# Splitting the last 344 tokens of a hybrid encoder layer into two parts of 172

## The chip, the cores and the metric

The kernel runs on one core of one Trainium2 chip, as one program. The metric is the device time of that program in microseconds (us); lower is better. The core has five engines that run side by side and wait for each other by semaphores: TensorE (PE, matrix products; its weight loads are shown apart as PEld), VectorE (DVE), ScalarE (ACT), GpSimd (POOL) and SyncE (SP, which here issues every transfer between HBM and the core). Products are written to eight banks of accumulator memory, each 128 partitions by 512 fp32 numbers.

## The reference, cut to what matters

One layer of an encoder trunk on 2048 prompt tokens and 32 sample tokens, model width 1024. The change touches only the very end of it, the second product of the feed-forward block, the residual sum and the final norm:

```
h = rmsnorm(x, norm_ffn_g) * (1 + sc2) + sh2
x = x + gt2 * (square(relu(h @ w_up)) @ w_down)      # w_up 1024 x 4096, w_down 4096 x 1024
y = rmsnorm(x, final_norm_g)

def rmsnorm(x, g):
    return x * rsqrt(mean(x * x, axis=-1) + 1e-6) * g
```

## The kernel before, in words

**Layout.** Everything is kept transposed: the 1024 model columns lie on the 128 partitions in eight tiles (`m` = 0 to 7), tokens run along the free axis. The feed-forward stage walks over three blocks of tokens (`b`), each made of two groups `g`. In the last block a group has 344 tokens; group 1 holds the end of the sequence with the 32 sample tokens, group 0 the 344 tokens before that. Group 1 is worked first, group 0 last, so it is group 0 that ends the program. Sums of the second product are kept in `acc[m][g]`.

**Precision by three products.** A fp32 operand is split into a high and a low part (`hi`, `lo`) of type fp32r, and a product is made of three matmuls (`mm3`, line 427, recorded by `mms`, profile line L414): high weights by high values, high by low, low by high. Each has its own load of a 128x128 tile of weights, even where two in a row use the same tile: 16000 loads for 16000 matmuls in the page.

**The hidden columns.** The 4096 hidden columns are taken in eight rounds `q`. Rounds before the last use a seven-product scheme; the last round of the last block (`ffn_last`, line 1875) is done plainly: for each group, each of the eight output tiles is the sum of 4 products of 3 matmuls, 12 matmuls of 344 columns, in one bank.

**After each output tile.** VectorE multiplies the bank by the gate and adds the sum so far (`stt`, L373); ScalarE squares it (`act`, L353); the squares of the tiles are added up into one tile (in group 0 by VectorE, `tt`, L368), except that for group 0 the squares of the last two tiles are kept apart.

**The last norm** (`final`, line 1936, and `rms_row`, line 859). The sum over the partitions is made on TensorE with the tile of squares as weights and a column of ones as values: a group of 344 is three pieces of 128 tokens, and each piece of each tile of squares shows up as two instructions, since here full fp32 is used. Three tiles of squares give 18 instructions. VectorE then scales the 128x3 result (`rcol`, L382), GpSimd raises it to the power of -0.5 (L368, POOL), TensorE turns each column back into a row over all partitions (`tr`, L425), and VectorE multiplies the eight tiles, already scaled by the norm's weights on ScalarE, by that row straight out of the bank. Tiles go out in three pairs and two single tiles (`dma`, L406).

**Banks.** `take` pops a bank from the front of a list of eight and `give` puts it back at the end. Following all calls from the start, the list stands at 1, 2, 0, 3, 6, 4, 5, 7 when `ffn_last` begins, and again when group 0 begins. The row sums and the row that comes back use the ring `M`, which holds bank 7 alone. Bank 7 is so the bank of the eighth output tile of each group, too.

**Order of work.** The program is recorded as a list of operations with what each reads and writes. A planner (`schedule`, line 246) then plays it through with an assumed cost for each operation, an assumed latency between engines, and a priority, and writes out a fixed order for each engine. Of the operations that are ready by its clock it takes the one with the lowest priority number (`LOCAL` 2, `EVAC` 3, which is the default, `GEMM` 4), and among equals the one that a later matmul needs first. Engines follow that order on the chip, whatever the real durations are. The assumed cost of one `mm3` is 3 * (0.443 n + 5) ns for n columns:

```python
self.mms([...], 3 * (0.443 * ps.n + 5))
```

Of the kernel before, what the change touches and what calls it, by code (L numbers as in the profile page):

```python
# [10 lines left out]
AF = mybir.ActivationFunctionType  # L11
ALU = mybir.AluOpType
# [4 lines left out]
P = 128  # L17
D = 1024
KT = 8
# [12 lines left out]
GB = [348, 348, 344]  # L32
FT = [0, 696, 1392]
G = 348
NB = 3
# [8 lines left out]
PE, DVE, ACT, POOL, DMA, NONE = range(6)  # L44
# [13 lines left out]
CHAIN, INV, LOCAL, EVAC, GEMM, IDLE = range(6)  # L58
# [280 lines left out]
class Kern:  # L339
# [1534 lines left out]

    def ffn_last(self, b, q, ops):

        w = {}
        for g, u in ((1, 0), (1, 1), (0, 0), (0, 1)):
            if u not in w:
                w[u] = [self.operand(self.wr, self.raw(self.raws, self.i["w_d"][2 * q + u, x])) for x in range(4)]  # L1880
            for i in range(2):
                for j in range(2):
                    m = 4 * i + 2 * u + j
                    ps = self.take(GB[b])
                    for e in range(2):
                        wh, wl = w[u][2 * i + e]
                        for k in range(2):
                            c = slice(256 * k + 128 * j, 256 * k + 128 * j + 128)
                            with self.p.at(GEMM):
                                self.mm3(ps[1], wh[:, c], wl[:, c], *ops[(e, g)][k], e == k == 0, e == k == 1)  # L1890
                    self.add(b, q, m, g, ps[1], last=True)
                    self.give(ps)
            if u == 1:
                self.final(b, g, self.ssq[g][1:])
        yield

    def ffn_plain(self, b, q, ops):

        for u in range(2):
            w = [self.operand(self.wr, self.raw(self.raws, self.i["w_d"][2 * q + u, x])) for x in range(4)]  # L1900
            for g in range(2):
                for i in range(2):
                    for j in range(2):
                        m = 4 * i + 2 * u + j
                        ps = self.take(GB[b])
                        for e in range(2):
                            wh, wl = w[2 * i + e]
                            for k in range(2):
                                c = slice(256 * k + 128 * j, 256 * k + 128 * j + 128)
                                with self.p.at(GEMM):  # L1910
                                    self.mm3(ps[1], wh[:, c], wl[:, c], *ops[(e, g)][k], e == k == 0, e == k == 1)
                        self.add(b, q, m, g, ps[1], first=True, last=True)
                        self.give(ps)
            if q == 7 and u == 1:
                for g in range(2):
                    self.final(b, g, self.ssq[g][1:])
            yield

    def square(self, b, m, g):

        end = (b, g) == (NB - 1, 0)
        a = self.acc[m][g][:, : GB[b]]
        if self.ssq[g] is None or self.ssq[g][0] != b:
            sa = self.piece("fs", b)
            self.ssq[g] = [b, sa]
            self.act(sa, a, AF.Square)
            return
        x = self.piece("fp" if end and m == 7 else "fx", b)
        self.act(x, a, AF.Square)
        sa = self.ssq[g][1]  # L1930
        if end and m in (6, 7):
            self.ssq[g].append(x)
        else:
            self.tt(sa, sa, x, ALU.add, DVE if end else POOL)

    def final(self, b, g, sq):
        w, ts = GB[b], self.span(b, g)
        end = (b, g) == (NB - 1, 0)
        if end:
            for m in range(KT):  # L1940
                a = self.acc[m][g][:, :w]
                self.act(a, a, AF.Copy, scale=self.nrm[:, 2, m : m + 1])
        r = self.rms_row(sq, w, None if end else sq[0])
        for m in range(KT):
            a, n = self.acc[m][g][:, :w], self.nrm[:, 2, m : m + 1]
            with self.p.at(GEMM):
                if end:
                    if m % 2 == 0:
                        y = self.slot((25, 26, 22, 23)[m // 2], 0, (P, 2, w))
                    self.tt(y[:, m % 2], a, r, ALU.mult)  # L1950
                    if m > 5:
                        self.dma(self.o["yT"][m, :, ts], y[:, m % 2])
                    elif m % 2:
                        self.dma(self.o["yT"][m - 1 : m + 1, :, ts].rearrange("m p t -> p m t"), y)
                    continue
                if m % 2 == 0 and (b < NB - 1 or m < 6):
                    self.tt(a, a, r, ALU.mult, POOL)
                    self.act(a, a, AF.Copy, scale=n)
                else:
                    self.stt(a, a, n, r, ALU.mult, ALU.mult)  # L1960
                with self.p.at(LOCAL):
                    self.dma(self.o["yT"][m, :, ts], a)
# [66 lines left out]
```

## Time and profile before

| | us |
|---|---|
| median of 3 runs | 2316.39 |
| lowest, highest | 2314.38, 2317.95 |
| the profiled execution, its own time | 2321.28 |
| its span, first to last instruction | 2319.5 |
| granted TensorE clock, mean | 0.996 |
| share of TensorE, VectorE, ScalarE, GpSimd in the span | 99%, 72%, 53%, 26% |

Rows of the timeline read: start in us from the span's start, duration in us, engine, line, operation, output <- input by the program's names, shape, how many were merged into the row (x), and in brackets how long the engine stood idle before and what ended it. `f` is a bank of the feed-forward products, `M` the bank of the row sums, `s` a working tile. Rows of groups read: line, engine, operation, names, shape, count, then busy us and mean ns of one. The matmul rows of the feed-forward stage all have one line, L414, so they are told apart by names and shapes.

### The profile page before, as it was taken

What the parts mean: (1) busy time and instruction counts of PE and PEld (TensorE: products, weight loads), DVE (VectorE), ACT (ScalarE), POOL (GpSimd) and SP (SyncE); (2) the same over time, 40 slices, a digit from 0 to 9 for tenths busy, and PEclk for the clock granted to TensorE, in tenths of its full rate; (3) what the DMA queues carried; (4) which work ended last, traced back from release to release, by engine and by line L of the source; (5) the groups of instructions that cost most, each with busy time, mean ns of one, the idle gap of its engine ahead of it and who ended that gap; (6) DMA issues with size and microseconds to landing.
All of it is one profiled execution on the core that took longest, in us unless ns stands there. A gap on an engine that the chain in (4) does not pass through costs nothing.

```text
span 2319.5 us, 45744 instructions
## 1 busy us (share of the span) xinstructions
PE 2294.0 (99%) x16000; PEld 2176.6 (94%) x16000; DVE 1664.7 (72%) x3618; ACT 1220.3 (53%) x2801; POOL 600.2 (26%) x846
## 2 busy tenths in 40 slices
PE   9999999999999999999999999999999999999998
PEld 6877778999999988999999999999999999999998
DVE  6656766577755545689999989776668886666775
ACT  5655656465664434476565545753344564344344
POOL 1124533224334023445444424210000250000001
PEclk9999999999999999999999999999999999999999
DMA  9488778465566766888777786997667897666771
GB/s 328 164 276 284 241 244 242 148 214 175 181 190 192 248 196 207 284 279 275 261 256 253 251 268 222 352 310 238 216 216 251 261 304 228 222 218 217 243 225 54
DMA packets 358328, 547.08 MB, mean 236 GB/s; under 512 B 66425, under 2 KB 182285, under 8 KB 358097
## 3 DMA queue, kind: packets, MB, share of 16 engines
q1 hardware_dynamic: 358096, 544.16, 72.3%
q8 instruction: 126, 2.06, 0.4%
q14 instruction: 106, 0.86, 0.1%
HBM read 390.96 MB, written 153.05 MB: 235 GB/s over the span
## 4 chain that ended last, share of the span: by engine, by line
PE 82%; DVE 6%; DMA 6%; ACT 2%; issue 2%; POOL 2%; SPq 1%; POOLq 0%; DVEq 0%; ACTq 0%
PE f L414 47%; PE g L414 25%; PE C L414 3%; DVE s L368 2%; PE L L414 2%; PE B L414 2%; DVE s L373 2%; ACT s L353 1%; POOL s L368 1%; PE M L414 1%; DVE wl L368 1%; DMA s<-th_d 1%; PE L L425 1%; DMA wr<-w_b 1%; SPq L406 1%
## 5 line engine op out<-in xcount | busy, mean ns | idle before, releaser
L353 ACT ACTIVATE s<-s 128x348 fp32r<-128x348 f32 (+13 forms) x1067 | 492.0, 485 | 333.6 <-DVE s L368 126.8
L414 PE MATMUL f<-s,wh 128*128 128x348 f32 (+1 forms) x2768 | 662.2, 322 | 0.3 <-DVE s L368 0.2
L414 PEld LDWEIGHTS f<-s,wh 128*128 128x128 f32 x2768 | 480.8, 188 | 2.6 <-DVE s L368 1.7
L368 DVE TENSOR_TENSOR s<-f,s 128x348 f32<-128x348 f32 (+1 forms) x696 | 348.2, 512 | 172.2 <-PE f L414 170.7
L414 PE MATMUL f<-s,wl 128*128 128x348 f32 (+1 forms) x1384 | 444.7, 321 | 0.0
L414 PE MATMUL g<-BH,wh 128*128 128x384 f32 (+2 forms) x1088 | 399.2, 367 | 0.7 <-ACT BH L353 0.4
L414 PE MATMUL g<-BH,wl 128*128 128x384 f32 (+2 forms) x1088 | 382.3, 351 | 0.0
L414 PE MATMUL g<-BL,wh 128*128 128x384 f32 (+2 forms) x1088 | 381.1, 350 | 0.4 <-DVE BL L373 0.4
L368 DVE TENSOR_TENSOR s<-s,s 128x348 fp32r<-128x348 f32 (+8 forms) x674 | 348.5, 546 | 37.5 <-ACT s L353 11.1
L414 PE MATMUL f<-BH,wh 128*128 128x348 f32 (+1 forms) x1024 | 330.0, 322 | 2.5 <-DVE s L373 1.9
L414 PE MATMUL f<-BL,wh 128*128 128x348 f32 (+1 forms) x1024 | 330.9, 323 | 0.0
L414 PE MATMUL f<-BH,wl 128*128 128x348 f32 (+1 forms) x1024 | 329.3, 322 | 0.0
L353 ACT ACTIVATE wh<-s 128x512 fp32r<-128x512 f32 x282 | 176.1, 632 | 233.6 <-PE f L414 199.9
L368 POOL TENSOR_TENSOR s<-s 64x15 f32<-64x15 f32 (+12 forms) x328 | 165.4, 504 | 465.1 <-issue 380.4
L368 POOL TENSOR_TENSOR s<-s,s 128x512 f32<-128x512 f32 (+5 forms) x153 | 191.0, 1257 | 289.9 <-ACT s L353 139.8
L414 PEld LDWEIGHTS f<-s,wl 128*128 128x128 f32 x1384 | 260.4, 188 | 0.0
L368 DVE TENSOR_TENSOR wl<-s,wh 128x512 fp32r<-128x512 f32 x282 | 220.2, 789 | 40.1 <-ACT wh L353 39.8
L414 PEld LDWEIGHTS g<-BH,wh 128*128 128x128 f32 x1088 | 205.1, 189 | 22.2 <-issue 3.6
L414 PEld LDWEIGHTS g<-BL,wh 128*128 128x128 f32 x1088 | 205.6, 189 | 17.4 <-DVE BL L373 1.1
L414 PEld LDWEIGHTS g<-BH,wl 128*128 128x128 f32 x1088 | 204.6, 188 | 18.2
L373 DVE SCALAR_TENSOR_TENSOR s<-s,s,s 128x384 f32<-128x384 f32 (+4 forms) x314 | 162.3, 538 | 54.7 <-ACT s L353 27.3
L414 PEld LDWEIGHTS f<-BH,wh 128*128 128x128 f32 x1024 | 192.9, 188 | 3.2 <-DVE s L373 2.2
(133 smaller groups left out, 3332.9 us busy)
## 6 DMA issues: line engine op xcount, KB each, us to landing
s<-w_u SPq DMA_DIRECT2D x124, 256.0 KB, 3.8
s<-w_d SPq DMA_DIRECT2D x121, 256.0 KB, 3.5
wh<-su_d SPq DMA_DIRECT2D x114, 256.0 KB, 3.9
wl<-su_d SPq DMA_DIRECT2D x114, 256.0 KB, 4.0
wh<-sd_d SPq DMA_DIRECT2D x100, 256.0 KB, 3.3
wl<-sd_d SPq DMA_DIRECT2D x100, 256.0 KB, 3.8
wr<-w_b SPq DMA_DIRECT2D x36, 512.0 KB, 5.4
s<-adaw SPq DMA_DIRECT2D x32, 512.0 KB, 6.1
```

Of the source, the lines that this page charges most:

```text
L353: self.p.op(ACT, c, lambda: nc.scalar.activation(out=R(out), in_=R(in_), func=func, **{k: R(v) for k, v in kw.items()}), [out, accum], [in ...
L368: self.p.op(eng, c, lambda: e.tensor_tensor(out=R(out), in0=R(a), in1=R(b), op=op), [out], [a, b])
L373: self.p.op(DVE, c, lambda: nc.vector.scalar_tensor_tensor(out=R(out), in0=R(a), scalar=R(s), in1=R(b), op0=op0, op1=op1), [out], [a, s, b])
L406: self.p.op(DMA, max(500, x), lambda: nc.sync.dma_start(out=R(out), in_=R(in_)), [out], [in_], lat=DMA_LATENCY + min(0, x - 500))
L414: nc.tensor.matmul(R(out), R(l), R(r), **kw)
L425: self.p.op(PE, 114, lambda: nc.tensor.transpose(R(out), R(in_), R(ident)), [out], [in_, ident])
```

## The change

In the last round of the last block, group 0 is no longer worked as 344 columns but as two parts of 172, one after the other: all eight output tiles of part A (tokens 0 to 171 of the group), then all eight of part B (172 to 343). Each part has its own squares, its own row sums and its own norm (`finish`), so it has 8 x 12 matmuls of 172 columns, and TensorE loads the same weight tiles once for each part. In each part the squares of all tiles but the last are added into one tile, and the last tile's square is kept apart, so there are two tiles of squares, each in two pieces (128 and 44 new tokens). Before part A begins, the list of eight banks is divided: the first four, 1, 2, 0, 3, become the ring `M` for the row sums, the other four, 6, 4, 5, 7, serve the products. The weights of both halves are requested ahead of the loop. Group 1 is worked as before.

```diff
-        for g, u in ((1, 0), (1, 1), (0, 0), (0, 1)):
...
+        w = [[self.operand(self.wr, self.raw(self.raws, self.i["w_d"][2 * q + u, x])) for x in range(4)] for u in range(2)]
+        for g, o, n in ((1, 0, GB[b]), (0, 0, 172), (0, 172, 172)):
+            sq = []
+            if (g, o) == (0, 0):
+                self.fbanks, self.banks["M"] = self.fbanks[4:], self.fbanks[:4]
+            for u, i, j in ((u, i, j) for u in range(2) for i in range(2) for j in range(2)):
+                m = 4 * i + 2 * u + j
+                ps = self.take(n)
...
+                        with self.p.at(GEMM):
+                            self.mm3(ps[1], wh[:, c], wl[:, c], hi[:, o : o + n], lo[:, o : o + n], e == k == 0, e == k == 1)
+                if g:
                     self.add(b, q, m, g, ps[1], last=True)
+                else:
+                    x = self.acc[m][0][:, o : o + n]
+                    self.stt(x, ps[1], self.modc[:, 5, m, 0:1], x, ALU.mult, ALU.add)
+                    t = self.new(("fk" if o else "fs") if not sq else "fr" if o else "fp" if m == 7 else "fx", (P, n))
+                    self.act(t, x, AF.Square)
+                    if sq and m != 7:
+                        self.tt(sq[0], sq[0], t, ALU.add)
+                    else:
+                        sq.append(t)
+                self.give(ps)
+            if g:
                 self.final(b, g, self.ssq[g][1:])
+            else:
+                self.finish(o, n, sq)
         yield
+
+    def finish(self, o, n, sq):
+        t0 = FT[NB - 1] + o
+        for m in range(KT):
+            x = self.acc[m][0][:, o : o + n]
+            self.act(x, x, AF.Copy, scale=self.nrm[:, 2, m : m + 1])
+        r = self.rms_row(sq, n, None)
+        for m in range(KT):
+            with self.p.at(GEMM):
+                if m % 2 == 0:
+                    y = self.slot((25, 26, 22, 23)[m // 2], 2 * o, (P, 2, n))
+                self.tt(y[:, m % 2], self.acc[m][0][:, o : o + n], r, ALU.mult)
+                if m > 5:
+                    self.dma(self.o["yT"][m, :, t0 : t0 + n], y[:, m % 2])
+                elif m % 2:
+                    self.dma(self.o["yT"][m - 1 : m + 1, :, t0 : t0 + n].rearrange("m p t -> p m t"), y)
```

What `square` and `final` did for group 0 of the last block (the branches on `end`) is taken out of them.

More of the change, by code (lines that the diff above doesn't have):

```diff
@@ L1875, in ffn_last @@
     def ffn_last(self, b, q, ops):
-        w = {}
-        for g, u in ((1, 0), (1, 1), (0, 0), (0, 1)):
[L1879 to L1890, printed above, removed]
-                    self.add(b, q, m, g, ps[1], last=True)
-                    self.give(ps)
-            if u == 1:
+        w = [[self.operand(self.wr, self.raw(self.raws, self.i["w_d"][2 * q + u, x])) for x in range(4)] for u in range(2)]
@@ new lines, in ffn_last @@
+        for g, o, n in ((1, 0, GB[b]), (0, 0, 172), (0, 172, 172)):
[5 more added lines that the diff above has]
+                ps = self.take(n)
+                for e in range(2):
+                    wh, wl = w[u][2 * i + e]
+                    for k in range(2):
+                        c = slice(256 * k + 128 * j, 256 * k + 128 * j + 128)
+                        hi, lo = ops[(e, g)][k]
+                        with self.p.at(GEMM):
+                            self.mm3(ps[1], wh[:, c], wl[:, c], hi[:, o : o + n], lo[:, o : o + n], e == k == 0, e == k == 1)
+                if g:
+                    self.add(b, q, m, g, ps[1], last=True)
+                else:
[9 more added lines that the diff above has]
+            if g:
@@ L1919, in square @@
     def square(self, b, m, g):
-        end = (b, g) == (NB - 1, 0)
         a = self.acc[m][g][:, : GB[b]]
@@ L1927, in square @@
             return
-        x = self.piece("fp" if end and m == 7 else "fx", b)
+        x = self.piece("fx", b)
         self.act(x, a, AF.Square)
         sa = self.ssq[g][1]
[L1931 to L1934, printed above, removed]
+        self.tt(sa, sa, x, ALU.add, POOL)
     def final(self, b, g, sq):
         w, ts = GB[b], self.span(b, g)
[L1938 to L1943, printed above, removed]
+        r = self.rms_row(sq, w, sq[0])
         for m in range(KT):
@@ L1946, in final @@
             with self.p.at(GEMM):
[L1947 to L1955, printed above, removed]
                 if m % 2 == 0 and (b < NB - 1 or m < 6):
```

## The prediction

> **What bounds the kernel now.** I read the page's first part, then the chain of work that ended last in order of time, then busy time by stretches, then the timeline of the last 30 us.
>
> ```profile
> span 2319.5 us, 45744 instructions
> PE 2294.0 (99%) x16000; PEld 2176.6 (94%) x16000; DVE 1664.7 (72%) x3618; ACT 1220.3 (53%) x2801; POOL 600.2 (26%) x846
> ```
> ```profile
> 2149.94 144.15 PE f L414 x913
> ...
> 2312.91 2.54 DVE s L368 x6
> ```
> ```profile
> 2290.60:2306.90 16.30, 16.29 (x107) 15.98 (x105) 11.08 (x20) 9.40 (x19) 5.67 (x6) 1.00 0.25 88
> 2306.90:2319.50 12.60, 3.19 (x21) 2.71 (x21) 4.21 (x10) 1.34 (x3) 0.86 (x1) 0.60 0.32 112
> ```
>
> See that TensorE sets the pace until about 2307 and that then a chain of small steps runs alone: in the last stretch no engine is busy for more than 4.21 of 12.60 us (columns: PE, PEld, DVE, ACT, POOL, then granted clock). The chain's 144 us piece is products of the feed-forward stage, its last piece the multiplications of the norm. Both stretches are touched by the change: group 0's products, and the chain behind them.
>
> ```profile
> 2290.62 0.47 PE L414 MATMUL f<-s,wh 128*128 128x344 f32 x2
> ```
> ```profile
> 2293.92 0.72 PE L414 MATMUL M<-ones,s 128*128 128x1 f32 x6
> 2296.96 0.49 PE L425 MATMUL M<-ident,rcol 128*128 128x128 f32 x3
> 2297.21 0.56 PE L414 MATMUL f<-s,wh 128*128 128x344 f32 x2
> 2297.49 0.46 ACT L353 ACTIVATE s<-M 128x344 f32<-128x344 f32 x1 [0.44 <-PE M L425]
> ```
> ```profile
> 2306.57 0.32 PE L414 MATMUL f<-s,wl 128*128 128x344 f32 x1
> 2306.93 0.57 DVE L373 SCALAR_TENSOR_TENSOR s<-f,modc,s 128x344 f32<-128x344 f32 x1 [0.90 <-PE f L414]
> 2307.54 0.49 ACT L353 ACTIVATE s<-s 128x344 f32<-128x344 f32 x1 [0.37 <-DVE s L373]
> 2307.55 2.21 PEld L414 LDWEIGHTS M<-ones,s 128*128 128x128 f32 x18 [0.95 <-DVE s L373]
> 2309.89 0.16 DVE L382 TENSOR_SCALAR rcol<-M 128x3 f32<-128x3 f32 x1 [2.38 <-PE M L414]
> 2310.13 0.86 POOL L368 TENSOR_TENSOR rcol<-rcol,mhalf 128x3 f32<-128x3 f32 x1 [8.84 <-DVE rcol L382]
> 2311.04 0.90 PE L425 MATMUL M<-ident,rcol 128*128 128x128 f32 x3 [1.19 <-POOL rcol L368]
> 2311.98 3.47 DVE L368 TENSOR_TENSOR s<-s,M 128x344 f32<-128x344 f32 x8 [1.93 <-PE M L425]
> ```
> ```profile
> 2315.64 0.58 SPq L406 DMA_DIRECT2D yT<-s  x1
> ```
>
> Group 0 runs on TensorE from 2290.62 to the start of its last matmul at 2306.57: 15.95 us for 96 product matmuls, group 1's 6 row sums and its 3 turned columns. Call T the end of the last product, 2306.57 + 0.32 = 2306.89. All 18 row-sum instructions wait for VectorE to leave the last product's bank, because the row sums use that same bank 7: 12 of them have had their squares earlier. The multiplications by the row end at 2311.98 + 3.47 = 2315.45, T + 8.56; the last transfer is issued at 2315.64 and the span ends 4.05 us after the last multiplication.
>
> **The change, part by part.**
>
> **1. Narrower matmuls.** 96 matmuls of 344 columns become 192 of 172, each with its own load of 128x128 weights. What one then costs decides the sum. First and last of unbroken runs:
>
> ```profile
> 78.77 0.28 PE L414 MATMUL g<-wl,BH 128*128 128x260 f32 x1
> ...
> 85.88 0.29 PE L414 MATMUL g<-wh,BL 128*128 128x260 f32 x1
> ```
> ```profile
> 2267.92 0.32 PE L414 MATMUL f<-BH,wh 128*128 128x344 f32 x1
> ...
> 2271.55 0.32 PE L414 MATMUL f<-BH,wl 128*128 128x344 f32 x1
> ```
>
> At 260 columns there are 60 matmuls with starts over 7.11 us, 59 steps of 0.1205 us; at 344 columns 24 over 3.63 us, 23 steps of 0.158 us. That is a straight line of 0.44 ns a column, and it would put 172 columns at 0.081 us. But the load can't be ignored any more:
>
> ```profile
> L414 PEld LDWEIGHTS f<-s,wh 128*128 128x128 f32 x2768 | 480.8, 188 | 2.6 <-DVE s L368 1.7 <-ACT s L353 0.5
> L414 PEld LDWEIGHTS g<-wh,BL 128*32 128x32 f32 x16 | 1.7, 108 | 0.1
> L414 PEld LDWEIGHTS B<-wl,modc 128*2 128x2 f32 x32 | 1.4, 84 | 0.0
> ```
> ```profile
> 2307.55 0.86 PEld L414 LDWEIGHTS M<-ones,s 128*128 128x128 f32 x7 [0.95 <-DVE s L373]
> ```
> ```profile
> 2294.48 0.30 PEld L414 LDWEIGHTS f<-s,wh 128*128 128x128 f32 x2
> ```
>
> A load takes 84, 108 and 188 ns for 2, 32 and 128 columns of weights: 0.83 ns a column, so some 107 ns of streaming in a load of 128. The row sums, whose matmul has one column, show the rate that loads alone allow: 7 loads in 0.86 us, the last 0.19 long, six steps of 0.112 us. Two loads of product weights follow each other at 0.30 - 0.19 = 0.11 us. So below about 240 columns the load binds: a matmul of 172 columns can't step faster than 0.107 us and, by the row at 260, not slower than 0.1205. I take 0.115: near the row sums, where loads alone bind, with a little for a matmul that really streams 172 columns beside the load.
>
> [...]
>
> From the start of group 0 TensorE then has 192 product matmuls, 6 row sums of group 1, and 8 of part A (two tiles of squares, two pieces, two instructions): 206 x 0.115 = 23.7 us. Turned columns cost about 0.08 each in mid-stream (2296.96 to 2297.21 for 3); 3 + 2 of them make 0.4. Together 24.1 against 15.95: +8.15. The last matmul is 0.08 shorter (0.32 at 344, 0.28 at 260, so 0.24). T moves by +8.1; with 0.107 by +6.4, with 0.1205 by +9.2.
>
> **2. The chain behind T**, at 172 tokens:
>
> ```profile
> L373 DVE SCALAR_TENSOR_TENSOR s<-f,modc,s 128x344 f32<-128x344 f32 x24 | 13.5, 570 | 4.7 <-PE f L414 4.7
> L373 DVE SCALAR_TENSOR_TENSOR s<-f,modc,s 128x32 f32<-128x32 f32 x20 | 4.8, 241 | 0.0
> L368 DVE TENSOR_TENSOR s<-s,M 128x344 f32<-128x344 f32 x8 | 3.5, 506 | 1.9 <-PE M L425 1.9
> L368 DVE TENSOR_TENSOR s<-C,s 128x128 f32<-128x128 f32 x65 | 15.7, 281 | 0.0
> ```
> ```profile
> L353 ACT ACTIVATE s<-s 128x344 f32<-128x344 f32 x128 | 62.4, 489 | 38.1 <-DVE s L368 20.0 <-DVE s L373 14.4 <-POOL rcol L368 1.5
> L353 ACT ACTIVATE s<-s 128x32 f32<-128x32 f32 x7 | 1.5, 234 | 0.2
> ```
> ```profile
> L368 POOL TENSOR_TENSOR s<-s,mhalf 128x2 f32<-128x2 f32 x33 | 24.8, 759 | 111.1 <-DVE s L368 71.7 <-DVE s L382 39.4
> ```
>
> Between the shapes shown: gate and sum 0.39 (570 and 241 ns), square 0.35 (489 and 234), each with 0.04 of hand-over, so the last square is ready at T + 0.82. The four row sums of the first tile of squares no longer share a bank with a product and run before that; four remain, 0.5 us (six take 0.72) plus 0.2 for load and hand-over: T + 1.5. Scaling 0.16 and 0.08; the power 0.70 (0.86 for three columns; two take 0.76 in the mean of runs with VectorE beside); 0.05; two turned columns 0.66 (three take 0.90); 0.04: T + 3.2. Eight multiplications: now 0.42 apart, less 172 x 1.04 ns (506 and 281 ns) = 0.244 apart, 7 x 0.244 + 0.33 = 2.0: T + 5.25 against T + 8.56, so -3.3. The two turned columns may run at full clock, as TensorE has been idle for less (now 0.60 granted in the stretch): up to 0.3 less.
>
> **3. Transfers.** 13 issues on SP become 18; part A's five lie below part B's products. At the end the multiplications finish 0.244 apart while the last issue takes 0.58, so the last waits for its forerunner: +0.2. Landing I leave as it is, 4.05 us after the last multiplication: half the bytes, as many rows, no shown change.
>
> **4. Work moved under part B.** Part A's 8 sums, adds, squares, scalings and multiplications: VectorE has about 0.39 + 0.33 + 0.33 = 1.05 us per output tile, against 12 x 0.115 = 1.38 of TensorE. It fits, at nothing. If that cover is thin, some of A's multiplications stand in VectorE's queue behind the last gate-and-sum and before B's scaling: the planner prices a matmul of 172 at 81 ns, so by its clock B ends early. Eight at 0.244 end at T + 2.4, and the scaling could be 0.9 later. I take 0 and keep 0.9 for the range. Group 1's final work, the earlier request for weights (same order, same places) and four banks for row sums cost nothing: TensorE waits for none of them in the rows shown.
>
> **Sum.** +8.1 - 3.3 + 0.2 = +5.0 us. The profiled execution took 2321.28 us (span 2319.5 and 1.8 around it), 4.9 above the median; it would become 2326.3. Against the median of 2316.39 that gives 2321.4 us. Bounds: +6.4 - 3.3 - 0.3 = +2.8, and +9.2 - 3.3 + 0.2 + 0.9 = +7.0.
>
> **The rivals.**
>
> *The load stays hidden (not slower).* If the step follows the line of columns, 192 x 0.081 = 15.6, with 14 row sums at 0.112 and 0.4 17.6, against 15.95 and 0.08: +1.55 - 3.1 = -1.5, 2314.9 us. The point at which it decides is a step of 0.09. For it speaks the straight line down to 260 columns; against it the row sums, whose matmul is the shortest and which still step at 0.112. [...]
>
> *Four banks make TensorE wait.* Bank 7 still carries group 1's norm and is the fourth bank of part A. Group 1's row is read out of it by 2297.49 + 0.46 = 2297.95, 7.3 us after 2290.62. Part A's fourth tile is due after 3 x 1.38 + 0.7 = 4.8 us. Kept in that order, TensorE waits 2.5 us: 2323.9. Against it: the planner knows the wait and can take the fifth to seventh tile first, whose banks are free, 3 x 1.38 = 4.1 us of work.
>
> *The chain does not shorten,* because part A's leftovers fill the engines behind T: +8.1, 2324.5.
>
> **How the numbers follow.** No change can be told from this kernel's noise within 0.2%, 4.6 us. The forecast's mechanism gets 0.78 (load 0.107 to 0.1205; the 4.6 us lie a little below its middle, so 0.6 of it is slower), the hidden load 0.08, the bank wait 0.10, the unshortened chain 0.04. Slower: 0.47 + 0.14 = 0.61; same 0.31 + 0.06 = 0.37; faster 0.02. The range goes from the lower bound, 2319.2, less 0.6 for the scatter of medians, to just short of the unshortened chain.
>
> **What would show it.** Matmuls of 128x172 with starts 0.115 us apart and loads without gaps; group 0 lasting 24 us; the chain from last product to last multiplication 5.2 us; 8 row sums for each part, four of B's before its last square. Steps of 0.09 or less would make the forecast wrong, as would a gap on TensorE ahead of part A's fourth tile.

## The result, and the profile after

The changed kernel takes 2321.79 us in the median of 14 runs (2317.07 to 2327.45), the kernel before 2317.36 in 14 runs beside them (2313.2 to 2321.39). The ratio is 1.0018, 95% interval 1.0011 to 1.0026: 4.2 us slower, between 2.5 and 6.0. The forecast was +5.0 us.

Single executions scatter by 8 to 10 us, more than any step of this change is worth, and the two profiled executions come to the point G below 4.1 us apart, though the change touches nothing ahead of it. So their spans (2319.5 and 2319.3 us) can't be compared. They are compared from a point that they share: the last gate-and-sum of group 1, which VectorE does in two pieces of 312 and 32 tokens. From it (G) to the start of the last product matmul (L), and on to the end (spans are printed to 0.1 us, so the last two lines hold to 0.05):

| us | before | after | difference |
|---|---|---|---|
| G | 2290.82 | 2286.70 | |
| G to L | 15.75 | 23.10 | +7.35 |
| last product: its duration | 0.32 | 0.27 | -0.05 |
| end of last product to start of last scaling (`rcol`) | 3.00 | 2.30 | -0.70 |
| ... to end of last multiplication | 8.56 | 5.80 | -2.76 |
| end of last multiplication to end of span | 4.05 | 3.43 | -0.62 |
| G to end | 28.68 | 32.60 | +3.92 |

The last line agrees with the ratio's 4.2 us. The time went into the stretch from G to L: the page of the changed kernel has 95 more matmul records and 4.6 us more busy TensorE.

```profile
span 2319.3 us, 45988 instructions
PE 2298.6 (99%) x16095; PEld 2181.1 (94%) x16095; DVE 1666.6 (72%) x3642; ACT 1223.5 (53%) x2817; POOL 598.8 (26%) x847
```

In its timeline the first two rows below are part of one unbroken run of group 0's matmuls, the others are the tail:

```profile
2296.29 0.39 PE L414 MATMUL f<-s,wh 128*128 128x172 f32 x2
...
2299.97 0.39 PE L414 MATMUL f<-s,wh 128*128 128x172 f32 x2
```
```profile
2286.70 0.70 DVE L373 SCALAR_TENSOR_TENSOR s<-f,modc,s 128x312 f32<-128x312 f32 x2 [1.18 <-PE f L414]
```
```profile
2309.80 0.27 PE L414 MATMUL f<-s,wl 128*128 128x172 f32 x1
2310.11 0.40 DVE L373 SCALAR_TENSOR_TENSOR s<-f,modc,s 128x172 f32<-128x172 f32 x1 [0.19 <-PE f L414]
2310.13 0.50 PE L414 MATMUL M<-ones,s 128*128 128x1 f32 x4
2310.42 2.03 DVE L368 TENSOR_TENSOR s<-s,M 128x172 f32<-128x172 f32 x8
2310.54 0.35 ACT L353 ACTIVATE s<-s 128x172 f32<-128x172 f32 x1 [0.52 <-DVE s L373]
2310.94 0.61 PE L414 MATMUL M<-ones,s 128*128 128x1 f32 x4 [0.31 <-ACT s L353]
2312.37 0.15 DVE L382 TENSOR_SCALAR rcol<-M 128x2 f32<-128x2 f32 x1
2312.60 0.70 POOL L368 TENSOR_TENSOR rcol<-rcol,mhalf 128x2 f32<-128x2 f32 x1 [4.28 <-DVE rcol L382]
2313.36 0.43 PE L425 MATMUL M<-ident,rcol 128*128 128x128 f32 x2 [1.81 <-POOL rcol L368]
2313.83 2.04 DVE L368 TENSOR_TENSOR s<-s,M 128x172 f32<-128x172 f32 x8 [1.30 <-PE M L425]
```
```profile
2311.02 5.88 SPq L406 DMA_DIRECT2D yT<-s  x10
```
```profile
2316.50 0.40 SPq L406 DMA_DIRECT2D yT<-s  x1
```

Between the first two rows lie 11 groups of three matmuls: 3.68 us for 33 steps, 0.1115 us a step, where 344 columns took 0.158. The matmul became half as wide and 29% cheaper. In the tail, see two rows of eight multiplications: the first (2310.42) is part A's, and it stands between part B's last gate-and-sum and part B's scaling. The last row sums are done at 2310.94 + 0.61 = 2311.55; the scaling has no idle time in brackets, it simply comes after part A's eight, 0.8 us later. All ten transfers, part A's five among them, are issued behind the last product, from 2311.02 on. TensorE waits for nothing while it works on group 0; its only wait up to 2311 is the short one for the last square:

```profile
PE M L414 <- ACT s L353: 0.3, 1, 0.3
```

### The profile page after: what moved, and what is told of

It is laid out like the page before. It is cut to its first block, busy times and chain, and to the rows that moved or that the text cites. A ratio compares the mean times of both kernels' runs of the same rounds, so it can differ in the third digit from the quotient of the medians.

```text
span 2319.3 us, 45988 instructions
## 1 busy us (share of the span) xinstructions
PE 2298.6 (99%) x16095; PEld 2181.1 (94%) x16095; DVE 1666.6 (72%) x3642; ACT 1223.5 (53%) x2817; POOL 598.8 (26%) x847
## 4 chain that ended last, share of the span: by engine, by line
PE 47%; DVE 3%; DMA 2%; issue 1%; ACT 1%; POOL 1%; SPq 0%; POOLq 0%; DVEq 0%
PE f L414 47%; DVE s L368 2%; DMA s<-x_d 1%; ACT s L353 1%; DMA s<-th_d 1%; DVE wl L368 0%; POOL s L368 0%; DVE s L373 0%; DMA yT<-s 0%; ACT wh L353 0%; DMA s<-w_u 0%; POOL rcol L368 0%; DVE BL L368 0%; PE M L414 0%; ACT BH L353 0%
## 5 line engine op out<-in xcount | busy, mean ns | idle before, releaser
L414 PE MATMUL f<-s,wh 128*128 128x348 f32 (+2 forms) x2824 | 668.3, 320 | 1.4 <-ACT s L353 0.6
L353 ACT ACTIVATE s<-s 128x348 fp32r<-128x348 f32 (+14 forms) x1075 | 493.0, 483 | 328.9 <-DVE s L368 127.8
L414 PEld LDWEIGHTS f<-s,wh 128*128 128x128 f32 x2824 | 488.2, 188 | 4.0 <-DVE s L368 2.7
L414 PE MATMUL f<-s,wl 128*128 128x348 f32 (+2 forms) x1412 | 451.1, 319 | 0.0
L414 PEld LDWEIGHTS f<-s,wl 128*128 128x128 f32 x1412 | 265.9, 188 | 0.0
```

Of the source, the lines that this page charges most:

```text
L353: self.p.op(ACT, c, lambda: nc.scalar.activation(out=R(out), in_=R(in_), func=func, **{k: R(v) for k, v in kw.items()}), [out, accum], [in ...
L414: nc.tensor.matmul(R(out), R(l), R(r), **kw)
```

## The experiments

All stage times below are read as in the table, from one trace of each kernel; "over before" is G to end less 28.68. The last column compares whole executions; "one execution" is too few for that.

| kernel | G to L | last product to last multiplication | to end | G to end | over before | measured ratio to before (95%) |
|---|---|---|---|---|---|---|
| before | 15.75 | 8.56 | 4.05 | 28.68 | | |
| changed | 23.10 | 5.80 | 3.43 | 32.60 | +3.92 | 1.0018 (1.0011 to 1.0026) |
| four banks alone | 16.44 | 7.62 | 4.04 | 28.42 | -0.26 | 1.0005 (0.9995 to 1.0015) |
| wide products | 15.75 | 7.60 | 4.11 | 27.78 | -0.90 | 1.0001 (0.9991 to 1.0011) |
| the same, fewer issues | 15.75 | 7.87 | 4.58 | 28.52 | -0.16 | 0.9998 (0.9989 to 1.0007) |
| true price | 23.29 | 5.34 | 3.35 | 32.25 | +3.57 | 1.0018 (1.0009 to 1.0026) |
| one bank | 25.29 | 6.21 | 3.42 | 35.19 | +6.51 | 1.0033 (1.0020 to 1.0046) |
| half load | 17.13 | 5.88 | 3.50 | 26.75 | -1.93 | one execution |
| double loads | 82.24 | 5.80 | 3.45 | 91.91 | +63.2 | one execution |
| 216 and 128 | 28.72 | 4.51 | 3.46 | 37.10 | +8.42 | 1.0038 (1.0024 to 1.0051) |
| 188 and 156 | 23.29 | 4.91 | 3.31 | 31.78 | +3.10 | one execution |
| 200 and 144 | 23.28 | 4.80 | 3.31 | 31.67 | +2.99 | one execution |

**Does the load bind the narrow matmul? Half the load.** Columns and matmuls as in the changed kernel, 64 columns of weights for 128.

```diff
+                        out = ps[1]
+                        if g == 0:
+                            c, out = slice(c.start, c.start + 64), out[:64]
...
-                            self.mm3(ps[1], wh[:, c], wl[:, c], hi[:, o : o + n], lo[:, o : o + n], e == k == 0, e == k == 1)
+                            self.mm3(out, wh[:, c], wl[:, c], hi[:, o : o + n], lo[:, o : o + n], e == k == 0, e == k == 1)
...
-                    self.stt(x, ps[1], self.modc[:, 5, m, 0:1], x, ALU.mult, ALU.add)
+                    self.stt(x[:64], ps[1][:64], self.modc[:64, 5, m, 0:1], x[:64], ALU.mult, ALU.add)
```

> The changed kernel, with only the first 64 of each 128 columns of weights loaded and used in group 0's last round, so half of that round's output rows are left out (their sums keep the earlier rounds). The matmuls are as many and still stream 172 columns. Theory (the load of 128 columns binds): the step falls from 0.1115 us to the line of columns, 0.082 to 0.085 us, and the time from the last gate-and-sum of group 1 to group 0's last product from 23.1 to 17.3 to 18 us. Rival (a floor per matmul, whatever is loaded): the step stays 0.11 us, 23.1 us.

```profile
2305.85 0.32 PE L414 MATMUL f<-s,wh 128*64 128x172 f32 x2
...
2308.70 0.32 PE L414 MATMUL f<-s,wh 128*64 128x172 f32 x2
```

Twelve groups of three lie between these rows: 2.85 us for 36 steps, 0.079 us, a little below the line of columns (0.081). G to L falls to 17.13 us, a little below the 17.3 to 18 expected. The load of 128 columns binds, not a floor per matmul, and without it the split would have gained: 1.93 us below before by the stages of this trace.

**The same from the other side: double the loads.** Each product of 172 columns made of two of 86.

```diff
-                            self.mm3(ps[1], wh[:, c], wl[:, c], hi[:, o : o + n], lo[:, o : o + n], e == k == 0, e == k == 1)
+                            for a, z in ((0, n),) if g else ((0, 86), (86, 172)):
+                                self.mm3(ps[1][:, a:z], wh[:, c], wl[:, c], hi[:, o + a : o + z], lo[:, o + a : o + z], e == k == 0, e == k == 1, skip_group_check=True)
```

> The changed kernel, each product of group 0 made of two matmuls of 86 columns where it had one of 172: twice the loads, the same columns. Theory (each load costs 0.1115 us whatever streams): 192 more steps, 21.4 us more, 44.5 us from group 1's last gate-and-sum to group 0's last product. Rival (time goes by columns, with a fixed 0.005 us a matmul): about 1 to 2 us more.

(Two accumulations are begun in one bank here, and the sums of that round come out different, the layer's output by a relative 0.052; the instructions are those named.) The stretches of its trace, with the granted clock behind the five engines:

```profile
2291.00:2292.00 1.00, 1.00 (x11) 1.00 (x11) 0.00 (x0) 0.00 (x0) 0.67 (x1) 1.00 0.00 0
2292.00:2293.00 1.00, 1.00 (x9) 1.00 (x8) 0.40 (x1) 0.54 (x2) 0.00 (x0) 0.75 0.00 0
2293.00:2294.00 1.00, 1.00 (x7) 1.00 (x6) 0.00 (x0) 0.25 (x1) 0.00 (x0) 0.50 0.05 16
```
```profile
2289.78 0.40 PE L414 MATMUL f<-s,wh 128*128 128x86 f32 x2
...
2292.12 0.40 PE L414 MATMUL f<-s,wh 128*128 128x86 f32 x2
...
2293.08 0.63 PE L414 MATMUL f<-s,wh 128*128 128x86 f32 x2
...
2294.36 0.63 PE L414 MATMUL f<-s,wh 128*128 128x86 f32 x2
```

The step came out as expected while it lasted: seven groups of three from 2289.78 to 2292.12, 21 steps of 0.1114 us, at 86 columns the same as at 172. The total did not, by 40 us: at 2292.5, 3.3 us after group 0 began (2289.20), the granted clock fell to 0.50 and stayed there, and the step went to 0.213 us (2293.08 to 2294.36, six steps). No engine made TensorE wait; all loads and matmuls follow each other without a gap. This was not among the theories.

**Parts of 216 and 128.** This run was meant to show the shorter end of a narrower last part. It also has the planner's true price (below), and its tiles on their way out lie elsewhere.

```diff
-        for g, o, n in ((1, 0, GB[b]), (0, 0, 172), (0, 172, 172)):
+        for g, o, n in ((1, 0, GB[b]), (0, 0, 216), (0, 216, 128)):
...
```

> The changed kernel with the planner's true price, and parts of 216 and 128 tokens where it had 172 and 172; tiles on their way out are placed elsewhere, so that nothing waits for them. Theory (below 240 columns a matmul costs its load): the same 23.2 us from group 1's last gate-and-sum to group 0's last product, and a shorter end, as part B is narrower (one piece of row sums, one turned column): 4.6 us from last product to last multiplication, 7.5 to the end where the changed kernel has 9.2; 2 us above before. Rival (steps follow the columns): 216 columns take 0.101 us or more and 128 less than 0.09.

```profile
2301.37:2304.79 3.42, 3.42 (x34) 3.42 (x32) 1.54 (x5) 1.82 (x7) 0.70 (x1) 1.00 0.15 51
2304.79:2308.20 3.41, 3.41 (x19) 3.41 (x18) 1.67 (x6) 1.23 (x4) 0.00 (x0) 0.50 0.02 5
```
```profile
2302.78 1.00 PE L414 MATMUL M<-ones,s 128*128 128x1 f32 x8
```
```profile
2303.00:2303.50 0.50, 0.50 (x6) 0.50 (x6) 0.00 (x0) 0.10 (x1) 0.00 (x0) 1.00 0.00 0
...
2304.50:2305.00 0.50, 0.50 (x7) 0.50 (x5) 0.12 (x2) 0.37 (x2) 0.26 (x1) 0.79 0.00 0
2305.00:2305.50 0.50, 0.50 (x4) 0.50 (x4) 0.23 (x1) 0.34 (x1) 0.00 (x0) 0.50 0.00 0
```

The end is about as short as expected, 4.51 us to the last multiplication and 7.97 to the end (4.6 and 7.5 expected). But the 128-column part, which began at 2299.14 with steps of 0.1115 us, lost the clock at 2304.8 and ran the rest at half: 28.72 us from G to L for 23.2, and by the stages the slowest of the kernels that were executed more than once. So the loss doesn't need the two accumulations of the run before. See what stands in the 3.4 us before it: not 128-column matmuls alone, but 22 of them and part A's eight row sums, which load as much and stream one column each.

**Where does the clock fall? Parts of 188 and 156, and of 200 and 144.** Only the sizes differ from the last run, and where part B's tiles lie on their way out.

```diff
-(0, 0, 216), (0, 216, 128)
+(0, 0, 188), (0, 188, 156)      # and (0, 0, 200), (0, 200, 144)
```

> Parts of 188 and 156 tokens, with the planner's true price. [...] Theory (the granted clock falls when less than about half of the time streams columns): the clock stays at 1.00 to the last product, 23.2 us from group 1's last gate-and-sum to it. [...]

> Parts of 200 and 144 tokens, otherwise the same. [...] Theory (a limit at half): clock 1.00 to the end, 23.2 us. [...]

```profile
2305.23:2308.65 3.42, 3.42 (x33) 3.42 (x32) 1.81 (x6) 2.48 (x8) 0.10 (x1) 1.00 0.41 139
2308.65:2312.06 3.41, 3.41 (x34) 3.41 (x32) 2.35 (x9) 1.48 (x4) 0.60 (x1) 1.00 0.03 5
```
```profile
2307.28 0.99 PE L414 MATMUL M<-ones,s 128*128 128x1 f32 x8
```
```profile
2313.00:2316.00 3.00, 3.00 (x29) 3.00 (x28) 1.95 (x8) 1.89 (x5) 0.00 (x0) 1.00 0.64 205
```

The rows are from the 144-column part: full clock to its end. Both kernels take 23.3 us from G to L, where 23.2 was expected. By the prediction's straight line, 0.44 ns a column, 172 columns, which kept the clock, stream for an estimated 68% of a step of 0.1115 us, 156 for 62%, 144 for 57%, and 128, which lost it, for 51%. A limit between the last two does not follow, though, because of the row sums. The changes of the clock themselves show what to count.

In the traces of before and of the changed kernel the changes of the granted clock lie whole multiples of 3.413 us apart (before: 15.71, 1377.62, 1381.04 and 2309.46 us, 399, 1 and 272 of them; changed: 17.54 and 2314.71 us, 673), so take stretches of 3.41 us that end at such a point. Count matmuls by their start (the x of the rows above also counts those that reach into a stretch). Before the fall at 128 columns, 22 matmuls and eight row sums stream 2824 columns, 1.24 us or 36%. The fall at 86 columns comes behind 31 matmuls, 34%. The 144-column part has its eight row sums as well (first row): 23 matmuls and these stream 43%, and the clock stays. So in these runs the limit lies between 36 and 43% of such a stretch; 128 columns without row sums, 51%, were not run, and by this count would have kept the clock. Cut into such stretches from 20 us on, the traces of before and of the changed kernel say the same: of those begun at full clock, the ones that kept it stream 43% or more. Three are followed by a fall, all with gaps: 36% (before, 1374.21 to 1377.62 us, TensorE busy for 1.54 us), 18% (before, 2306.05 to 2309.46) and 3% (changed, 2311.29 to 2314.71). What the chip itself counts is not shown.

**The products left wide, the norm split.**

```diff
+        for g, o, n in ((1, 0, GB[b]), (0, 0, GB[b])):
...
+                    for sq, o, n in zip(sqs, (0, 172), (172, 172)):
+                        x = self.acc[m][0][:, o : o + n]
+                        self.stt(x, ps[1][:, o : o + n], self.modc[:, 5, m, 0:1], x, ALU.mult, ALU.add)
...
+                self.finish(0, 172, sqs[0])
+                self.finish(172, 172, sqs[1])
```

> The split undone for the products alone: 96 matmuls of 344 columns, then gate, squares, row sums and norm in two parts of 172, with the four banks for row sums. Theory: group 0 lasts 16 us again, the last multiplication ends 7.0 us behind the last product (5.8 in the changed kernel, 8.6 before), small last transfers save 0.5; 2 us below before, 6 below the changed kernel. Rival (what costs is the doubled work on VectorE, ScalarE and SP, not the matmuls): the time stays within 1 us of the changed kernel.

G to L is back at 15.75 us with all the doubled small work still there, so the 7.35 us are TensorE's own: about 6.3 for the narrow matmuls (191 steps of 0.1115 us against 95 of 0.158) and 0.9 for part A's eight row sums, which here stand behind the last product. The end gained less than expected, 7.60 us to the last multiplication instead of 7.0, since the row sums of the first tile wait for an addition on VectorE; and 4.11 behind it, because SP is late:

```profile
2306.41 3.98 DVE L368 TENSOR_TENSOR s<-s,M 128x172 f32<-128x172 f32 x16 [0.79 <-PE M L425]
```
```profile
2307.01 5.02 SPq L406 DMA_DIRECT2D yT<-s  x10
```

Ten issues take 5.02 us, 16 multiplications 3.98, so the last issue (2311.64) comes 1.25 us after the last multiplication. By stages the kernel is 0.9 us below before, where 2 was expected; measured it can't be told from it.

**The same with six issues.** Part A in two transfers of four tiles, part B in one of four, one of two, two of one.

```diff
-                if m % 2 == 0:
-                    y = self.slot((25, 26, 22, 23)[m // 2], 2 * o, (P, 2, n))
+                c = (2 if m > 3 else 4) if o else 4
+                if m % c == 0:
+                    y = self.slot((22 + m // 4 if o else 25 + m // 4), n * (m % 4), (P, c, n))
...
```

> Products of 344 columns and the norm in two parts of 172, as in the run before of that kind, but part A goes out in two transfers of four tiles and part B in one of four, one of two and two of one: 6 issues where there were 10. Theory (SP is behind at the end: its last issue comes 1.25 us after the last multiplication): last issue 0.4 us after the last multiplication, 0.8 us less than that kernel, 1.7 below before. Rival (larger first transfers hold up the last ones): no gain on that kernel.

```profile
2310.80 1.35 PE L425 MATMUL M<-ident,rcol 128*128 128x128 f32 x4 [0.59 <-POOL rcol L368]
```

A miss. The last issue stands at 2316.50, 8.85 us behind the last product as in the kernel before this one, and 0.98 us behind the last multiplication (2315.52), where 0.4 was expected. That multiplication itself comes 0.27 us later, for a reason that has nothing to do with the issues: behind the same chain, the four turned columns took 1.35 us here and 0.43 for each two there. (The changed kernel's two took 0.43 at a granted clock of 1.00, before's three 0.90 at 0.50.) And the span ends 3.6 us behind the last issue instead of 2.86, though the last transfer is as small. Fewer and larger transfers bought nothing; the rival is nearer, though what held SP and the landing is not settled. The ratio of 0.9998 leaves both kernels with wide products indistinguishable from before, so there is no version here that beats before by more than can be measured.

**Four banks alone.**

```diff
         for g, u in ((1, 0), (1, 1), (0, 0), (0, 1)):
+            if (g, u) == (0, 0):
+                self.fbanks, self.banks["M"] = self.fbanks[4:], self.fbanks[:4]
```

> One part alone: the kernel before, with its list of banks divided in front of group 0 (four for the row sums, four for products), products still 344 wide. Theory (narrow matmuls cost 7.3 us, the row sums' bank saves a little): group 0 lasts 15.9 to 16.1 us from first to last product matmul as before, 12 of 18 row sums run ahead of the last square, the scaling starts 2.1 us behind the last product instead of 3.0, and the time is 0.9 us below before. Rival (four product banks make TensorE wait): a gap of up to 2.5 us on TensorE in group 0 and a time 1 to 2 us above before.

```profile
2313.72 0.32 PE L414 MATMUL f<-s,wl 128*128 128x344 f32 x1
2313.88 0.72 PE L414 MATMUL M<-ones,s 128*128 128x1 f32 x6
2315.23 0.83 PE L414 MATMUL M<-ones,s 128*128 128x1 f32 x6 [0.63 <-ACT s L353]
2316.10 0.16 DVE L382 TENSOR_SCALAR rcol<-M 128x3 f32<-128x3 f32 x1 [1.44 <-PE M L414]
```

Six row sums now stand right behind the last product, only six wait for the last square, and the scaling starts 2.06 us behind the last product, as expected (2.1). But the other six moved in front of the last product and cost TensorE 0.69 us there: work that filled a wait at the end now fills the engine that sets the pace. What is left of the 0.94 us is 0.26, where 0.9 was expected. TensorE never waits for one of the four product banks.

**One bank.** The changed kernel without the division.

```diff
-            if (g, o) == (0, 0):
-                self.fbanks, self.banks["M"] = self.fbanks[4:], self.fbanks[:4]
```

> The changed kernel without the four banks for row sums: bank 7 alone serves them, and eight serve products. Theory: the last product of part B needs bank 7, from which part A's multiplications still read their row, so TensorE waits for all eight of them, 1 to 3 us; 1 to 2 us above the changed kernel, 5 to 6.5 above before. Rival (the four banks do nothing): within 0.5 us of the changed kernel.

```profile
2319.43 0.43 PE L414 MATMUL f<-s,wh 128*128 128x172 f32 x2 [1.93 <-DVE s L368]
```

In the middle of group 0's last product tiles TensorE waits 1.93 us for part A's multiplications, which read their row from bank 7. G to L grows by 2.2 us, the time to 6.5 over before by stages, within the measured interval. The four banks are needed once the norm runs beside products; alone they are worth little.

**The planner's true price.**

```diff
-                  (ps, wl, ah, dict(start=False, stop=last, **kw))], 3 * (0.443 * ps.n + 5))
+                  (ps, wl, ah, dict(start=False, stop=last, **kw))], 3 * max(0.443 * ps.n + 5, 112))
```

> The changed kernel, with the planner's price of a product raised to 0.112 us a matmul wherever it assumed less. Theory (the planner ends part B too early by its clock, so that part A's multiplications stand in front of part B's scaling): group 0 still 23.3 us, part A's eight multiplications end before the last gate-and-sum, last multiplication 5.0 us behind the last product instead of 5.8, 0.8 us below the changed kernel. Rival (the place of those multiplications costs nothing): within 0.2 us of the changed kernel.

```profile
2309.69 0.81 DVE L368 TENSOR_TENSOR s<-s,M 128x172 f32<-128x172 f32 x3
...
2313.15 0.40 DVE L373 SCALAR_TENSOR_TENSOR s<-f,modc,s 128x172 f32<-128x172 f32 x1 [0.19 <-PE f L414]
2314.70 0.16 DVE L382 TENSOR_SCALAR rcol<-M 128x2 f32<-128x2 f32 x1 [1.15 <-PE M L414]
```
```profile
2315.68 0.69 PE L425 MATMUL M<-ident,rcol 128*128 128x128 f32 x2 [1.10 <-POOL rcol L368]
```

Part A's last multiplications now end at 2310.5, before part B's last three gates-and-sums, and the scaling starts 1.59 us behind the last product instead of 2.30. Of the 0.71 us won, 0.26 went again: the two turned columns took 0.69 us for 0.43. G to L is 0.19 us longer. By stages the kernel is 0.35 us below the changed one, where 0.8 was expected; the runs can't tell the two apart.

## Why the prediction was right, point by point

The direction, the size and the place were right: slower by 4.2 us where 5.0 were forecast, with the cost on TensorE and the gain in the tail. Three terms made it, and all three were off, by 0.8, 0.5 and 0.8 us. That the second was off the other way brought the sum nearer to the measured one, which is luck.

*Narrower matmuls, +8.1 forecast, +7.3 measured.* The step was 0.1115 us where 0.115 was taken; 206 steps of 0.1115 and three turned columns make 23.2, less 15.95, the measured difference to 0.1. The prediction had all five turned columns in there; part A's two came only behind the last product (2309.91). The allowance "a little for a matmul that really streams 172 columns beside the load" was wrong: the step is 0.1114 at 86 columns and 0.1115 at 128, 172 and 216, the same as the row sums with one column (0.112). The half-load run shows that it is the load: 64 columns of weights load in 135 ns where 128 take 188, and the step is 0.079. The 107 ns that the prediction works out from the lengths of loads lie within 5 ns of the step.

*The chain behind the last product, -3.3 forecast, -2.76 measured.* The step that failed is in part 4: "I take 0 and keep 0.9 for the range". Part A's eight multiplications did stand before part B's scaling, for the reason given there, and cost 0.8 us; the run with the true price takes 0.71 of that away. The rest of the chain was 0.25 us shorter than worked out, as the two turned columns ran at full clock (0.43 us; granted 1.00 until 2314.71), which the prediction had allowed for. How fast they come looks like chance: with the true price they took 0.69 us, and the two kernels with wide products differ in it behind the same chain. Before's three ran at half clock (0.90 us, granted 0.50 from 2309.46 on, where three in mid-stream took 0.49 at 1.00), so some 0.4 of the 2.76 us is not the split's doing.

*Transfers, +0.2 forecast, -0.62 measured.* The step that failed is "landing I leave as it is". The last issue did slip, from 0.19 to 0.63 us after the last multiplication, but the span then ended 2.80 us after that issue, not 3.86. With tiles of 344 columns that distance is 3.86 and 3.84 (before, four banks alone); with 172 it is 2.7 to 2.9 in six kernels, but 3.6 in the one with six issues, so the cause of the shorter landing stays open. The prediction also had part A's five transfers below part B's products; they were issued behind them.

*Work moved under part B, 0 forecast, 0 measured on TensorE:* no wait on group 0's products. The rival in which four banks make TensorE wait did not come: the order written out takes the fifth to seventh tile of part A first, as argued against it. The rival with a hidden load fell by the half-load run, and the unshortened chain by the rows of the tail.

The kernel with parts of 216 and 128 lies above the range, for a reason that stood in none of the rivals: the fall of the clock.

## What to carry to other kernels

Each part of a matmul split along its columns loaded its weights again here (16095 loads for 16095 matmuls in the page), and that load set a floor: with 128 columns of fp32r weights, 344 columns took 0.158 us a step and 260 took 0.1205, but 216 took the same 0.1115 as 86, the price of the load. The straight line through 260 and 344 columns meets that price at an estimated 240. A split of the last work pays the added loads on the engine that sets the pace and wins a tail that is only as long as its chain, so price both from rows before halving; here 7.3 us bought 3.4. And a planner whose price has no floor for the load orders the small work for a machine that isn't there.

## What the runs showed of the hardware that was not expected

TensorE's granted clock fell from 1.00 to 0.50 though loads and matmuls followed each other without a gap: 3.3 us after group 0 began at 86 columns, and 5.6 us after the part began at 128 columns with eight row sums among them; at 144, 156 and 172 it stayed at 1.00 to the last product. What fits is the share of a 3.41 us stretch in which columns stream: 34 and 36% lost the clock, 43% kept it. The loads slowed down with it (192 ns for one at full clock, 333 at half, from their groups in the double-loads run), and the step of 0.1115 us became 0.213. Looking for gaps would not have warned here: time spent on loads behaved as gaps did, which lost the clock at 36% too (before, at 1377.62 us). The changed kernel was not at that edge among its products: its own stretch with part A's eight row sums (2304.47 to 2307.88) streams 49%.

From the last issue to the end of the span, tiles of 344 columns take 3.85 us and tiles of 172 mostly 2.8. The size of the very last transfer alone does not set this, as the kernel with six issues shows (3.6 us).
